# A two-layer gated encoder in fp32 on one core: a third plain block at the FFN's start, one-bank PSUM tiles for half products, other buffers and orders in the way down

## The chip, the cores and the metric

The kernel runs on one core of a Trainium2 chip. The metric is the device time of one execution in microseconds (us), the median of several runs. In a profile PE is TensorE (matmuls), PEld its weight loads, DVE is VectorE, ACT ScalarE, POOL GpSimd and SP SyncE; the last issues most of the DMAs. A core's matrix products go into PSUM, which has eight banks of 512 fp32 values in each of 128 partitions.

## The reference

Two sequences of 512 and 256 tokens with 1024 features go through two layers. A layer adds a mixer of four gated branches to x and then a feed-forward network (FFN) with a short convolution over the tokens. What bears on the change is the end of the mixer and the FFN:

```python
for l in range(2):
    ...
    x = x + merged @ w_out[l]                      # 1024 x 1024
    h = rms_norm(x, ffn_norm[l])
    u = depthwise_conv(h @ w_up[l], w_dw, b_dw)    # 1024 x 5632, three taps over tokens
    a, b = split(u)                                # 2816 columns each
    x = x + (silu(a) * b) @ w_down[l]              # 2816 x 1024
```

All of it is fp32. The kernel makes an fp32 product of three passes, with each operand split in a high part and a remainder.

## The kernel before, in words

Both sequences lie side by side as 768 columns (tokens); features lie on the 128 partitions, so x is eight tiles of 128 x 768. HALF is 384. A product of K blocks of 128 features takes 3K matmuls for each column segment (`fm`, L488): high by high, remainder by high, high by remainder. Weights come in units of 128 x 512 by DMA (`raw`, issued by SP), are rounded on ACT (`whi`, L434) and the remainder taken on DVE (`wlo`, L443).

PSUM tiles are of two kinds: `mm_ps()` gives a tile of two banks (two of them), `ps()` a tile of one bank (four of them). A tile is taken again when its last reader is done.

`proj_out` (the way out of the mixer): x tiles 0 to 3 get a full product each; tiles 4 to 7 get their product in two rounds, first columns 0 to 383, then 384 to 767. Products 0 and 1 of a round share a two-bank tile, and so do 2 and 3. DVE adds each to x (L1413). Behind each round `hnorm` normalises that half: squares on ACT, sums on POOL, column sums and a broadcast by two small matmuls on PE (L580, L592), then for each of the eight tiles a scaling (L602) and a split into `hh` (ACT, L616) and `hl` (DVE, L618).

The FFN has 22 blocks j, each a pair of 128-column products (columns j and 22 + j of w_up), which go through the convolution (L1443 on ACT, L1437 and L1439 on DVE, four DVE rows for a product), tanh (L1547), a DVE step (L1549), a multiplication on POOL (L1550) and a split (L1552 on ACT, L1554 on DVE). The pairs are of two kinds:

- A plain block is two products over all 1024 features and both halves: 96 matmuls of 384 columns. Blocks 0 and 1 are plain (`ffn_plain`). While PE does them, `t_gen` and `t3_gen` make the inputs T1 to T4 of the other kind on DVE and ACT, from the normalised x. ACT copies each half product out of PSUM (L1457).
- The others go by Strassen-like sums, seven half products for the pair (`ffn_seven`): 84 matmuls. The first, X, is copied out (L1510) and accumulated into again. The seventh (T4) is put off to `ffn_rest`, which runs inside the next pair behind its second product, or inside a way down.

`FF_SEQ` is the order of pairs ("u", j) and ways down ("d", first block, blocks): a way down multiplies two or four finished blocks by their rows of w_down, for all eight x tiles. Each result is copied to a `y` buffer (L1585; three buffers) and added to x in DRAM (`xsp`) by an accumulating DMA that POOL issues (L1564). A way down of two blocks is eight products of 12 matmul pairs. The last way down of a layer takes x from DRAM and adds on the chip: in layer 0 in two rounds by `lagged` (columns 0 to 511, then 512 to 767; DVE adds at L1372 and next layer's norm work follows), in layer 1 by a whole product, an addition (L1603) and a store (L1604) for each x tile.

The instruction order on each engine is fixed at build time by a planner's clock: generators queued with a due time (`go_fast`) put their instructions in when PE's counted time passes it. `b()` gives a tile of 128 x 768 from a pool of 24, `s()` one of six.

Of the kernel before, what the change touches and what calls it, by code (L numbers as in the profile page):

```python
# [21 lines left out]
SEQS = ((0, 4), (4, 2))  # L22
GATE_ORDER = (2, 1, 3, 0)
NFF = 22
FF_PLAIN = 2
HALF = NT // 2

FF_SEQ = (("u", 0), ("u", 1), ("u", 2), ("u", 3), ("d", 0, 2), ("u", 4), ("u", 5), ("u", 6), ("d", 2, 4), ("u", 7),
          ("u", 8), ("u", 9), ("u", 10), ("d", 6, 4), ("u", 11), ("u", 12), ("u", 13), ("u", 14), ("d", 10, 4),
          ("u", 15), ("u", 16), ("u", 17), ("u", 18), ("u", 19), ("d", 14, 2), ("u", 20), ("u", 21), ("d", 16, 2),  # L30
          ("d", 18, 4))
# [216 lines left out]
class Net:  # L248
# [1139 lines left out]
    def proj_out(self):  # L1388
        nc = self.nc
        self.xs = []  # L1390
        self.norm_begin()
        self.xg = {0: [], HALF: []}
        src = self.xin if self.l == 0 else self.xsp
        for m in range(8):
            x = self.b()
            nc.sync.dma_start(out=x, in_=src[m])
            self.xs.append(x)
        for m in range(8 - self.LAG):
            p = self.mm_ps()
            self.fm(self.halves(p), self.units(2, 128), self.mg, rel=4)  # L1400
            self.add_x(p, self.xs[m], m)
            self.sq_in(m, self.xs[m], 0, HALF)
            self.sq_in(m, self.xs[m], HALF, NT)
            self.go_fast(self.save_x(m, self.xs[m], 0, NT), 2.0)
        jobs = [(m, self.units(2, 128)) for m in range(8 - self.LAG, 8)]
        for c0 in (0, HALF):
            for i, (m, us) in enumerate(jobs):
                if i % 2 == 0:
                    p = self.mm_ps()
                pp = p[:, 512 * (i % 2):512 * (i % 2) + HALF]  # L1410
                self.fm(((pp, c0, c0 + HALF),), us, self.mg, 4 if c0 else 0)
                x = self.xs[m][:, c0:c0 + HALF]
                nc.vector.tensor_add(x, x, pp)  # L1413
                self.sq_in(m, self.xs[m], c0, c0 + HALF)
                self.go_fast(self.save_x(m, self.xs[m], c0, c0 + HALF), 1.5)
            self.hnorm(c0, 3.0, self.f("fn"))

    def lagged(self, jobs, g, fin):

        self.drain()  # L1420
        for c0, c1 in ((0, NS), (NS, NT)):
            for i, (m, us, xs, x, rel) in enumerate(jobs):
                if i % 2 == 0:
                    pp = self.mm_ps()
                p = pp[:, 512 * (i % 2):512 * (i % 2) + 512]
                self.fm(((p[:, 0:c1 - c0], c0, c1),), us, xs, rel if c0 else 0)
                self.x_update(p[:, 0:c1 - c0], x, m, g, c0, c1)
                fin(m, x, c0, c1)
# [30 lines left out]
    def ffn_plain(self):  # L1459
# [1 line left out]
        cols = [c + j for j in range(FF_PLAIN) for c in (0, NFF)]  # L1461
        n = 3
        wts = [self.units(2, 128) for _ in cols]
        zs = [self.b() for _ in cols]
        self.finish(0)
        for w, z in zip(wts[:n], zs):
            self.plain_half(z, 0, w)
# [12 lines left out]
        self.run_out(e)  # L1480
        for j in range(FF_PLAIN):
            self.go_fast(self.ffn_block(j, *zs[2 * j:2 * j + 2]), 1.0 + 9.0 * j)

    def ffn_block(self, j, z1, z2):
        u = []
# [71 lines left out]
    def ffn(self):  # L1557
# [10 lines left out]
        for step in FF_SEQ[FF_PLAIN:]:  # L1568
# [8 lines left out]
            if step != FF_SEQ[-1]:  # L1577
                for m in range(8):
# [2 lines left out]
                    if o == 0:  # L1581
                        us = self.units(1, 128)
                    self.fm(self.full(p), us, xs, n * int(o + n == 4), o)
                    y = self.pm.tile([128, NT], F32, tag="y", name=self.nm("y"), bufs=3)
                    nc.scalar.copy(y, p[:, 0:NT])  # L1585
                    self.go_fast(add(m, y), 1.0)
                    if o + n == 4:
                        self.ffn_rest()
                continue
            self.ffn_rest()  # L1590
            self.drain()
# [6 lines left out]
            if last_l:  # L1598
                self.drain()
                for m in range(8):  # L1600
                    p = self.mm_ps()
                    self.fm(self.full(p), self.units(1, 128), xs, 4)
                    nc.vector.tensor_add(xx[m], xx[m], p[:, 0:NT])  # L1603
                    nc.sync.dma_start(out=self.out[m], in_=xx[m])  # L1604
                continue
            jobs = [(m, self.units(1, 128), xs, xx[m], 4) for m in range(8)]
            self.norm_begin()
# [135 lines left out]
```

## Time and profile before

| | |
|---|---|
| runs, us | 2838.42, 2837.56, 2827.6; median 2837.56 |
| profiled execution, us | 2834.98, its span 2833.2 |
| busy, us of the span | PE 2729.4 (96%), DVE 1781.7 (63%), ACT 1151.5 (41%), POOL 689.7 (24%) |
| mean granted clock of PE | 0.984 of full speed |

Busy times are sums over instructions; a matmul's end is modelled, so PE's 96% is not 96% of its best rate. An engine's idle time costs something only where PE waits for it.

### The profile page before, as it was taken

To read this page: it belongs to the slowest core of one execution; us is meant where nothing else is said; L and a number is where in the kernel's file an instruction comes from. 1 tells how busy PE (TensorE), PEld (TensorE's weight loads), DVE (VectorE), ACT (ScalarE), POOL (GpSimd) and SP (SyncE) were. 2 spreads that over 40 slices of the span, in tenths; PEclk is the share of its full clock that TensorE was granted. 3 is DMA by queue.
4 is the path that set the end of the run, shared out by engine and by line. 5 is a ranking of instruction groups with operands and counts; after the bars stand their busy time and mean duration, and the time that the engine had idled before them with its cause. 6 is when DMAs were issued, how large, how long until landed. Compare 5 with 4: busy or idle time off the path is not lost. (4 is left out here: it accounts for less than half of the span.)

```text
span 2833.2 us, 40110 instructions
## 1 busy us (share of the span) xinstructions
PE 2729.4 (96%) x15196; PEld 2468.4 (87%) x15196; DVE 1781.7 (63%) x3046; ACT 1151.5 (41%) x2349; POOL 689.7 (24%) x584
## 2 busy tenths in 40 slices
PE   9999999999998899999899999999999988999999
PEld 8778988888898799998787789888888987999988
DVE  6644347786338767868546443477864386678674
ACT  6443333223225445545444433332232254455452
POOL 3402113121121332233215021131211213322331
PEclk9999999999999999999999999999999999999999
DMA  4101113221141454344621111131212413543445
GB/s 161 42 27 38 43 48 114 61 67 60 60 143 48 88 117 96 97 101 113 171 90 42 27 38 42 49 114 60 67 60 60 140 51 87 118 96 97 102 108 156
DMA packets 129793, 233.71 MB, mean 82 GB/s; under 512 B 18496, under 2 KB 36288, under 8 KB 129600
## 3 DMA queue, kind: packets, MB, share of 16 engines
q1 hardware_dynamic: 115776, 193.40, 21.6%
q0 software_dynamic: 13824, 37.75, 8.2%
q8 instruction: 119, 1.95, 0.3%
q14 instruction: 74, 0.61, 0.1%
HBM read 174.33 MB, written 55.20 MB: 81 GB/s over the span
## 5 line engine op out<-in xcount | busy, mean ns | idle before, releaser
L443 DVE TENSOR_TENSOR wlo<-raw,whi 128x512 fp32r<-128x512 f32 (+1 forms) x576 | 456.4, 798 | 116.6 <-ACT whi L434 97.7
L488 PE MATMUL mm<-b,whi 128*128 128x256 f32 (+2 forms) x1920 | 439.9, 343 | 39.1 <-DVE b L1554 13.7
L434 ACT CAST whi<-raw 128x512 fp32r<-128x512 f32 (+1 forms) x576 | 346.4, 613 | 232.2 <-PE mm L488 79.6
L488 PE MATMUL ps<-b,whi 128*128 128x384 f32 (+1 forms) x1472 | 362.4, 342 | 32.6 <-ACT s L1510 26.0
L488 PEld LDWEIGHTS mm<-b,whi 128*128 128x128 f32 x1920 | 315.7, 192 | 77.7 <-DVE b L1554 16.2
L512 PE MATMUL mm<-whi,hh 128*128 128x512 f32 (+2 forms) x752 | 312.4, 415 | 6.8 <-ACT hh L537 5.7
L488 PE MATMUL mm<-hh,whi 128*128 128x512 f32 (+1 forms) x1152 | 302.1, 343 | 0.0
L488 PEld LDWEIGHTS ps<-b,whi 128*128 128x128 f32 x1472 | 255.3, 191 | 48.2 <-ACT s L1510 28.0
L488 PE MATMUL mm<-hh,wlo 128*128 128x512 f32 (+1 forms) x1152 | 296.8, 338 | 0.0
L488 PE MATMUL mm<-hl,whi 128*128 128x512 f32 (+1 forms) x1152 | 294.8, 337 | 0.0
L512 PE MATMUL mm<-whi,hl 128*128 128x512 f32 (+2 forms) x752 | 278.8, 371 | 0.3 <-DVE hl L544 0.2
L512 PE MATMUL mm<-wlo,hh 128*128 128x512 f32 (+2 forms) x752 | 278.2, 370 | 0.0
L488 PE MATMUL ps<-hh,whi 128*128 128x384 f32 x768 | 259.2, 338 | 7.3 <-ACT s L1516 4.4
L488 PE MATMUL mm<-b,wlo 128*128 128x512 f32 (+2 forms) x960 | 264.5, 340 | 0.0
L488 PE MATMUL ps<-hl,whi 128*128 128x384 f32 x768 | 258.9, 337 | 1.3 <-DVE hl L618 1.3
L488 PE MATMUL ps<-hh,wlo 128*128 128x384 f32 x768 | 257.7, 336 | 0.0
L519 POOL TENSOR_TENSOR st<-st,mhalf 128x16 f32<-128x16 f32 (+5 forms) x50 | 94.9, 1897 | 599.0 <-DVE st L1002 374.7
L488 PE MATMUL ps<-b,wlo 128*128 128x384 f32 (+1 forms) x736 | 230.2, 341 | 0.0
L1356 POOL TENSOR_TENSOR b<-b,b 128x768 f32<-128x768 f32 x48 | 100.2, 2087 | 463.4 <-DVE b L1351 447.1
L512 PEld LDWEIGHTS mm<-whi,hh 128*128 128x128 f32 x752 | 177.1, 236 | 29.2 <-issue 12.8
L488 PEld LDWEIGHTS mm<-hh,whi 128*128 128x128 f32 x1152 | 177.3, 189 | 26.6 <-issue 3.3
L488 PEld LDWEIGHTS mm<-hh,wlo 128*128 128x128 f32 x1152 | 176.2, 188 | 24.4
(230 smaller groups left out, 4811.9 us busy)
## 6 DMA issues: line engine op xcount, KB each, us to landing
raw<-wu SPq DMA_DIRECT2D x560, 256.0 KB, 2.7
xsp<-y POOLq DMA_DIRECT2D x96, 384.0 KB, 6.0
b<-xsp SPq DMA_DIRECT2D x24, 384.0 KB, 6.0
do<-ot SPq DMA_DIRECT2D x36, 132.0 KB, 1.8
b<-do SPq DMA_DIRECT2D x12, 384.0 KB, 3.5
raw<-wu SPq DMA_DIRECT2D x16, 208.0 KB, 4.0
b<-xin SPq DMA_DIRECT2D x8, 384.0 KB, 6.5
xsp<-b SPq DMA_DIRECT2D x8, 384.0 KB, 2.5
```

The source lines that it names most:

```text
L434: self.nc.scalar.copy(hi, raw)
L443: self.nc.vector.tensor_sub(lo, raw, hi.bitcast(F32))
L488: nc.tensor.matmul(ap, w, x[:, c0:c1], start=(k == 0 and i == 0 and not more), stop=(k == K - 1 and i == 2), skip_group_check=more)
L512: nc.tensor.matmul(ap, x[:, cols], w, start=(k == 0 and i == 0), stop=(k == 7 and i == 2))
L519: self.nc.gpsimd.tensor_tensor(r, ms, self.mhalf[:, 0:n], op=ALU.pow)
L1356: nc.gpsimd.tensor_add(a, a, t)
```

## The change

The third block becomes plain: `FF_PLAIN` is 3, and in `FF_SEQ` the first way down comes behind pair 4 in place of pair 3. The two products of block 2 lie in two of the three `y` buffers. In `proj_out` and `lagged` every half product gets a one-bank tile. `ffn_rest` is called behind every product of a way down; it does something at the first call only, so in a way down of two blocks the put-off seventh product comes behind the first x tile, before behind the second. In the last way down but one, d(16, 2), copies 1 to 7 go to `b()` tiles. In layer 1 the last two x tiles are finished, added and stored in two pieces, 512 and 256 columns.

```diff
-FF_PLAIN = 2
+FF_PLAIN = 3
...
-FF_SEQ = (("u", 0), ("u", 1), ("u", 2), ("u", 3), ("d", 0, 2), ("u", 4), ("u", 5), ("u", 6), ("d", 2, 4), ("u", 7),
+FF_SEQ = (("u", 0), ("u", 1), ("u", 2), ("u", 3), ("u", 4), ("d", 0, 2), ("u", 5), ("u", 6), ("d", 2, 4), ("u", 7),
...
             for i, (m, us) in enumerate(jobs):
-                if i % 2 == 0:
-                    p = self.mm_ps()
-                pp = p[:, 512 * (i % 2):512 * (i % 2) + HALF]
+                pp = self.ps()[:, 0:HALF]
...
             for i, (m, us, xs, x, rel) in enumerate(jobs):
-                if i % 2 == 0:
-                    pp = self.mm_ps()
-                p = pp[:, 512 * (i % 2):512 * (i % 2) + 512]
+                p = self.ps()
...
-        zs = [self.b() for _ in cols]
+        zs = [self.b() for _ in cols[:4]] + [self.y() for _ in cols[4:]]
...
-                    y = self.pm.tile([128, NT], F32, tag="y", name=self.nm("y"), bufs=3)
+                    y = self.b() if step == FF_SEQ[-2] and m else self.y()
                     nc.scalar.copy(y, p[:, 0:NT])
                     self.go_fast(add(m, y), 1.0)
-                    if o + n == 4:
-                        self.ffn_rest()
+                    self.ffn_rest()
...
+                    for c0, c1 in ((0, NS), (NS, NT)):
+                        p = self.ps()
+                        self.fm(((p[:, 0:c1 - c0], c0, c1),), w, xs, 4 * int(c0 > 0))
+                        nc.vector.tensor_add(xx[m][:, c0:c1], xx[m][:, c0:c1], p[:, 0:c1 - c0])
+                        nc.sync.dma_start(out=self.out[m, :, c0:c1], in_=xx[m][:, c0:c1])
```

Below `FF_PLAIN` the lines of the changed kernel lie a few lines lower or higher (L1411 for L1413, L1453 for L1457, L1584 for L1585, L1563 for L1564, L1549 for L1550, L1546 for L1547, L1551 for L1552). In the order of instructions the change shows as follows; behind a row stands whose semaphores it waits for (`Activation` is ACT). First PE in layer 0's second round of `proj_out`: the ones-matmul of the first half's norm, the starts of products 2 and 3 (tiles `mm` or `ps`, `b` is the merged branches, `whi` the weights), and the first plain product (from `hh` and `hl`). Before:

```order
L592 MATMUL ps_7763<-s_7749,ones 128x384 [waits DVE_49]
...
L488 MATMUL mm_7773<-b_6634,whi_7412 128x384
L488 MATMUL mm_7773<-b_6635,whi_7412 128x384
...
L488 MATMUL mm_7773<-b_6634,whi_7481 128x384 [waits DVE_49]
L488 MATMUL mm_7773<-b_6635,whi_7481 128x384
...
L488 MATMUL ps_7893<-hh_7256,whi_7550 128x384 [waits DVE_49,Activation_49]
```

And now:

```order
L592 MATMUL ps_7766<-s_7752,ones 128x384 [waits DVE_49]
...
L488 MATMUL ps_7776<-b_6634,whi_7412 128x384 [waits PE_49]
L488 MATMUL ps_7776<-b_6635,whi_7412 128x384
...
L488 MATMUL ps_7830<-b_6634,whi_7481 128x384
L488 MATMUL ps_7830<-b_6635,whi_7481 128x384
...
L488 MATMUL ps_7899<-hh_7256,whi_7550 128x384 [waits DVE_49,Activation_49]
```

Product 3 has a tile of its own and no wait for DVE; the order is the same.

Second, ACT in the first way down of two blocks: the copies into y (`DMASW` is a wait for one of the accumulating stores, counted from the first), with what stands between them. Before:

```order
L1585 COPY y_8588<-mm_8562 128x768 [waits PE_49]
L434 CAST whi_8603<-sum_8518 128x512 [waits DVE_49]
L1585 COPY y_8606<-mm_8590 128x768 [waits PE_49]
L434 CAST whi_8625<-raw_8434 128x512
L1536 ACTIVATE s_8398<-ps_8399 128x384 [waits PE_49]
L1443 ACTIVATE s_8641<-s_8398,fc_80 128x768 [waits DVE_49,Activation_49]
L1585 COPY y_8653<-mm_8628 128x768 [waits PE_49]
L434 CAST whi_8668<-raw_8480 128x512 [waits DMAHW4_49,DVE_49]
L1547 ACTIVATE s_8398<-s_8561 128x768 [waits DVE_49,Activation_49]
L1585 COPY y_8674<-mm_8655 128x768 [waits DMASW0_49,PE_49]
L1585 COPY y_8698<-mm_8676 128x768 [waits DMASW1_49,PE_49]
```

And now:

```order
L1546 ACTIVATE y_7894<-s_8628 128x768 [waits DVE_49,Activation_49]
L1584 COPY y_8737<-mm_8708 128x768 [waits PE_49]
...
L1535 ACTIVATE s_8532<-ps_8533 128x384 [waits PE_49]
L1439 ACTIVATE s_8768<-s_8532,fc_80 128x768 [waits DVE_49,Activation_49]
...
L1584 COPY y_8782<-mm_8757 128x768 [waits PE_49]
L1551 ACTIVATE b_8729<-y_7894 128x768 [waits Pool_49]
L1546 ACTIVATE s_8532<-s_8707 128x768 [waits DVE_49,Activation_49]
L1584 COPY y_8809<-mm_8784 128x768 [waits DMASW0_49,PE_49]
L434 CAST whi_8824<-raw_8614 128x512 [waits DMAHW0_49]
L1584 COPY y_8829<-mm_8811 128x768 [waits DVE_49,PE_49]
L1584 COPY y_8851<-mm_8831 128x768 [waits DMASW1_49,PE_49]
```

`y_7894` is a product of block 2, which is still being gated. The wait for the first store stands at the third copy, one sooner, and the fourth waits for DVE's last step on `y_7894`.

Third, POOL in the last way down but one, d(16, 2) of layer 0: the stores and the multiplication of the last block. Before:

```order
L1564 DMA xsp<-y_12553 128x768 [waits DMASW0_49,Activation_49]
L1564 DMA xsp<-y_12571 128x768 [waits DMASW1_49,Activation_49]
L1564 DMA xsp<-y_12616 128x768 [waits DMASW2_49,Activation_49]
L1550 TENSOR_TENSOR s_12377<-s_12377,s_12604 128x768 [waits DVE_49,Pool_49]
L1564 DMA xsp<-y_12637 128x768 [waits DMASW3_49,Activation_49]
```

And now:

```order
L1563 DMA xsp<-y_12548 128x768 [waits DMASW0_49,Activation_49]
L1563 DMA xsp<-b_12591 128x768 [waits DMASW1_49,Activation_49]
L1549 TENSOR_TENSOR s_12372<-s_12372,s_12577 128x768 [waits DVE_49,Pool_49]
L1563 DMA xsp<-b_12614 128x768 [waits DMASW2_49,Activation_49]
L1563 DMA xsp<-b_12634 128x768 [waits DMASW3_49,Activation_49]
```

The multiplication stands one store sooner, and the stores from the second on read tiles of the large pool.

## Rows read from the trace of the kernel before

**Rows 1.** PE's waits, whole span: us in total, times, longest us
```profile
PE ps L488 <- ACT s L1510: 26.0, 6, 5.5
PE mm L488 <- DVE b L1554: 13.7, 8, 2.8
PE mm L488 <- DVE b L1413: 10.1, 8, 2.9
...
PE mm L488 <- ACT y L1585: 6.5, 4, 3.6
PE mm L488 <- DVE b L1372: 5.9, 8, 1.2
...
PE ps L488 <- DVE b L1413: 2.9, 2, 2.1
```

**Rows 2.** Busy time by engine in one stretch of layer 0's FFN
```profile
core 0: us, PE busy (x) PEld busy (x) DVE busy (x) ACT busy (x) POOL busy (x), PEclk, DMA share, GB/s
895.50:938.30 42.80, 31.28 (x166) 29.60 (x164) 40.48 (x62) 24.61 (x43) 10.13 (x6) 0.96 0.18 56
```

**Rows 3.** The same of three short stretches (PEclk: granted clock)
```profile
850.30:857.10 6.80, 6.00 (x19) 6.00 (x20) 6.80 (x10) 3.47 (x7) 3.30 (x2) 0.50 0.21 65
1379.40:1382.80 3.40, 3.05 (x8) 1.86 (x6) 0.31 (x1) 0.80 (x1) 0.85 (x1) 0.50 1.08 281
2267.40:2274.20 6.80, 4.46 (x24) 4.14 (x24) 6.80 (x11) 3.53 (x7) 3.29 (x2) 1.00 0.23 68
```

**Rows 4.** PE in order of time, way out of the mixer
```profile
851.10 1.01 PE L488 MATMUL mm<-b,whi 128*128 128x384 f32 x2 [2.91 <-DVE b L1413]
```

**Rows 5.** DVE in order of time, the same place
```profile
845.62 1.70 DVE L602 SCALAR_TENSOR_TENSOR b<-b,fc,ssq 128x384 f32<-128x384 f32 x2 [0.42 <-ACT ssq L596]
...
858.35 0.56 DVE L1413 TENSOR_TENSOR b<-b,mm 128x384 f32<-128x384 f32 x1 [1.25 <-PE mm L488]
...
859.35 1.84 DVE L618 TENSOR_TENSOR hl<-b,hh 128x384 fp32r<-128x384 f32 x2
```

**Rows 6.** PE in order of time: layer 0's first pairs, kernel's end
```profile
897.53 0.51 PE L488 MATMUL ps<-b,whi 128*128 128x384 f32 x2
...
904.64 0.79 PE L488 MATMUL ps<-b,whi 128*128 128x384 f32 x2 [4.86 <-ACT s L1510]
...
938.29 0.62 PE L488 MATMUL mm<-b,whi 128*128 128x512 f32 x2 [2.79 <-DVE b L1554]
...
2794.55 0.98 PE L488 MATMUL mm<-b,whi 128*128 128x512 f32 x4 [0.89 <-ACT y L1585]
```

**Rows 7.** DVE in order of time: behind layer 0's plain products
```profile
904.42 0.74 DVE L1437 SCALAR_TENSOR_TENSOR s<-b,fc,s 128x511 f32<-128x511 f32 x1
...
906.78 0.69 DVE L443 TENSOR_TENSOR wlo<-sum,whi 128x512 fp32r<-128x512 f32 x1
...
914.73 2.35 DVE L1437 SCALAR_TENSOR_TENSOR s<-b,fc,s 128x511 f32<-128x511 f32 x1
...
937.30 0.94 DVE L1554 SCALAR_TENSOR_TENSOR b<-b,b 128x768 fp32r<-128x768 f32 x1
```

**Rows 8.** ScalarE (ACT) in order of time, layer 0, ahead of pair 5
```profile
977.04 1.03 ACT L1443 ACTIVATE s<-s,fc 128x768 f32<-128x768 f32 x1
980.61 0.48 ACT L1510 COPY s<-ps 128x384 f32<-128x384 f32 x1 [2.54 <-PE ps L488]
```

**Rows 9.** GpSimd (POOL) in order of time, a block's multiplication
```profile
914.29 2.23 POOL L1550 TENSOR_TENSOR b<-b,s 128x768 f32<-128x768 f32 x1 [13.89 <-DVE b L1549]
```

**Rows 10.** Line L1585 (ns min/median/max), and landings of L1564 stores
```profile
L1585 ACT COPY y<-mm x96: 774/800/804, 941.6 to 2797.5; 128x768 f32<-128x768 f32 x96
...
DMA to landing us min/median/max: 4.3/6.0/10.5
```

**Rows 11.** DMA issues: KB each, median us to landing
```profile
out<-b SPq DMA_DIRECT2D x8, 384.0 KB, 2.3
...
xsp<-b SPq DMA_DIRECT2D x8, 128.0 KB, 1.7
```

More of the change, by code (lines that the diff above doesn't have):

```diff
@@ L1482, in ffn_plain, with y @@
             self.go_fast(self.ffn_block(j, *zs[2 * j:2 * j + 2]), 1.0 + 9.0 * j)
+    def y(self):
+        return self.pm.tile([128, NT], F32, tag="y", name=self.nm("y"), bufs=3)
     def ffn_block(self, j, z1, z2):
@@ L1600, in ffn @@
                 for m in range(8):
[L1601 to L1604, printed above, removed]
+                    w = self.units(1, 128)
+                    if m < 6:
+                        p = self.mm_ps()
+                        self.fm(self.full(p), w, xs, 4)
+                        nc.vector.tensor_add(xx[m], xx[m], p[:, 0:NT])
+                        nc.sync.dma_start(out=self.out[m], in_=xx[m])
+                        continue
+                    for c0, c1 in ((0, NS), (NS, NT)):
[3 more added lines that the diff above has]
+                        nc.sync.dma_start(out=self.out[m, :, c0:c1], in_=xx[m][:, c0:c1])
                 continue
```

## The prediction

> **What bounds the kernel now.** I read the list of waits first, then the stretches around the two FFN openings, then single rows. TensorE (PE) is busy nearly all the time, so what counts is where it waits. Its list of waits [rows 1] names, for both layers together: 26.0 us for the copy of L1510 (a pair's first product leaving PSUM), 13.7 for L1554 (the last step of a gated block), 10.1 and 2.9 for the additions of L1413 (the way out of the mixer), 6.5 for the copies of L1585 (the way down) and 5.9 for L1372 (the end of a layer). All of these places are edited. Around 860 to 980 us, where layer 0 opens its FFN, the waits have one cause at a time. From the end of the plain products (first matmul of the next product but one at 897.53 less the 2.1 us of the product before it, so 895.45) to 938.3 PE is busy 31.3 of 42.8 us and VectorE (DVE) 40.5 [rows 2]: there DVE is the bound. Three stretches show what a wait costs beyond itself: PE ran at half clock (0.50) for 6.8 us after the 2.9 us wait at 851.10 [rows 4] and for 3.4 us near 1379, but not after the same wait in layer 1 (1.00) [rows 3]. A half-clock stretch costs half of PE's busy time in it: 3.0 and 1.5 us.
>
> The sum is made against the profiled execution, 2835.0 us (span 2833.2 and 1.8 around it). The median of the three runs, 2837.6, is 2.6 above it, inside their own spread of 10.8. About 0.5%, 14 us, is what a measurement of this kernel can tell from no change.
>
> **A. Half products of the way out in one-bank tiles.** Today products 1 and 3 of each round write the second half of a tile whose first half DVE still has to read. Eight waits cost 10.1 us, the longest (one per layer) 2.9, so the other six 0.72 on average [rows 1]. With a tile for each product, PE goes on at once; what it then meets is the normalised input of the first plain product. That chain runs on DVE from 845.62 to 861.2, 1.25 us of it waiting for PE's last product [rows 5], and is set off by a ones-matmul on PE, ahead of which three short waits (2.1 us) go. So it would run from 843.5 for 14.3 us to 857.8; the first plain product, whose last eighth and six one-column matmuls take about 0.9 us more, ends at 858.7. Before it starts when the addition at 858.35 ends and takes 24 matmuls and those six. One matmul takes 0.173 us: from 897.53 to the start of the wait that ends at 904.64 there are 2.25 us, less 0.17 for the last one's end, for twelve [rows 6]. That gives 863.8. Layer 0 gains 5.1. Layer 1 has no half clock to win (3.0 less) but a longer wait at the hand-over, 2.1 against 0.8 of the 2.9 [rows 1], so 1.3 more: 3.4. **A: -8.5**, between -4.3 (only the six short waits) and -16 (all of 10.1, 2.9 and 3.0).
>
> **B. A third plain block.** A pair by seven products takes 84 matmuls, plain 96. Twelve more at 0.173 are +2.1 us a layer. Against it stands the bound of the opening. DVE cannot start the first convolution before the plain products are done; today it starts 9.0 us behind them, at 904.42, as the transformed inputs (T1 to T4) still occupy DVE and ScalarE. From there it takes 33.8 us to the end of the L1554 at 937.30 that the first product of the way down needs [rows 7]; PE passes at 938.29 [rows 6]. With 16.6 us more plain products, the transformed inputs are ready before PE is; the first convolution starts 1.5 us behind PE (a copy and a 1.0 us scaling on ScalarE, [rows 8]). The same DVE work lies ahead of the way down, two pairs by seven and two blocks, and one more set of convolution rows of the third block, 2.4 us (904.42 to 906.78, [rows 7]). So 1.5 + 33.8 + 2.4 = 37.7 in place of 42.8: -5.1, net of the matmuls -3.0 a layer. **B: -6.0**, between +4.2 (DVE's lateness stays whole) and -24 (PE never waits there: 28 us in place of 42.8).
>
> POOL slows DVE in that stretch: while it multiplied from 914.29 to 916.5 [rows 9], the DVE row at 914.73 took 2.35 us in place of 0.74 [rows 7]. The Trainium skill (SBUF — State Buffer, "Who interferes with whom") has it that a DVE instruction with two SBUF inputs stands still for the whole of a GpSimd one that reads SBUF; the trace agrees, as that row ends 0.6 behind POOL's. By this rule a third block's multiplication in the same stretch would cost up to 2.2 us more a layer, and B would be -1.6; by the instruction order it falls behind the L1554 that counts, so B stays.
>
> **C. The third block's inputs lie in two of the three y buffers.** The way down of blocks 0 and 1 has eight copies into y, each followed by an accumulating store. Before, the fourth copy waits for the first store; now the third does, and the fourth for DVE to end block 2. Call the moment when PE passes the wait for L1554 R. Before, R = 938.3, and the X product of the pair after next ends as its copy starts, 980.6 [rows 8], so starts at 978.5; less the 14.6 us of the pair between, the way down with its stalls takes 25.6. Now POOL's queue has block 2's multiplication ahead of the first store. DVE reaches what that needs after some 15 rows, about 9 us (four of them the convolution set); POOL's multiplication takes 2 [rows 9], so the first store goes at R + 11 and lands 6.0 later, and the third copy (0.8) is over at R + 18 [rows 10]. PE, which without it would have needed the tile at R + 10, stands for 8 us, and has five products and copies still to go: the pair starts at R + 27. **C: +2.8** for both layers. Least: 0 waits, 16.6 us, -18. Most: a landing of 10.5 [rows 10] and a new half-clock stretch of 3.0, +18.
>
> **D. The seventh product one product sooner** is neutral in the other short way down, d(14,2): POOL's multiplication also moves one place up, ahead of the third store in place of behind it, so that store leaves later as the block is ready sooner; the y buffers go on setting the pace. 0, up to 2 us either way in a layer.
>
> **E. y copies of d(16,2) in the large pool.** Copies 1 to 7 no longer wait for a store. Of the 6.5 us for L1585, 3.6 (the longest [rows 1]) stand in layer 0 ahead of the last way down, followed by the half clock at 1379 (1.5 [rows 3]), and 0.9 in layer 1 [rows 6]. L1554 of the last pair, the next thing that PE needs, comes sooner too (it stood behind such a copy on ScalarE). **E: -6.0**, at least -2 if the loads of x, which need the stores, come late instead.
>
> **F. One-bank tiles at the end of layer 0**: 5.9 us of L1372 [rows 1] go. DVE's additions and splits take about as long as the 256-column products there, but four tiles let PE run ahead. **F: -5.9**, -3 to -9 (a half-clock stretch behind it may go as well).
>
> **G. Split last stores.** Behind the last matmul stand an addition of 768 columns, about the 0.94 us of the DVE row of that size at 937.30 [rows 7], and a store of 384 KB, 2.3 us. A third of the columns is left: 0.6 off the addition, and by the 128 KB row, 1.7, another 0.6 off the store [rows 11]. **G: -1.2**.
>
> **Sum**: -8.5 - 6.0 + 2.8 - 6.0 - 5.9 - 1.2 = -24.8; 2835.0 - 24.8 = 2810.
>
> **Rivals.**
> *The y buffers cost more.* For it speaks that stores in the way down have taken up to 10.5 us to land [rows 10] and that an 8 us stall is longer than any at these places so far (5.5 at most [rows 1]); against it, that the old stall at the next pair's X goes, which C counts. +7.5 us a layer on C: 2825.
> *DVE's lateness stays.* DVE is 40.5 of 42.8 busy and the third block brings it a full block of convolution and gating. If the first convolution is again 9 us late, B is +4.2: 2820. Against: the transforms run while PE has 16.6 us more to do.
> *All waits go.* If the block's y buffers come free in time and the first plain product finds its input, A, B and C go half of the way to their far ends, some -25 us more: 2785.
> *Slower.* If two y buffers stayed taken for the whole way down, each of the eight copies would wait for its predecessor's store, 0.8 + 6.0 = 6.8 us [rows 10], 54 us in place of 25.6, +29 a layer: 2866 with the other terms. It decides from about five such copies a layer: each costs 4.7 us more than PE's 2.1, the old way down has 9 us over its 16.6 to give, and the other terms 13.8 a layer. Against it: in the changed queue only the third and fourth copies wait on something new.
>
> **How the numbers follow.** Chances: forecast (2797 to 2822) 0.58; y buffers 0.16; DVE's lateness 0.12; all waits gone 0.09; slower 0.05. Faster by over 0.5% means below 2823.4: the forecast, all waits gone, most of DVE's lateness and a quarter of the y case, 0.80; within 0.5%: 0.15; slower 0.05. The range 2792 to 2826 leaves out the slower case, half of the all-gone case and some of the y case's far side, under 0.2. The likeliest case's own range is 2797 to 2822.
>
> **What would show it.** A: no PE wait for the additions of the way out, small waits for hl in the first plain product. B: the first convolution within 2 us of the last plain copy, and d(0,2) ready some 5 us sooner after the plain products. C: a PE wait of about 8 us for a y copy in the middle of d(0,2), none at the next pair's X. E, F: no PE wait for L1585 in d(16,2), none for x additions at the layer's end. Wrong it would be if the stall of C were twice as long, or if new half-clock stretches followed the small waits of A.

## The result, and the profile after

The changed kernel takes 2803.4 us (median of four runs, 2801.5 to 2810.3); the kernel before, run beside it, 2833.3 (2827.6 to 2838.4). The ratio is 0.990, 95% interval 0.987 to 0.9929. The profiled execution took 2802.0 with a span of 2800.2, so the span fell by 33.0 us against the profiled execution of before; the medians are 29.9 apart.

PE's waits over the whole span now (us in total, times, longest), to be held against [rows 1]:

```profile
PE ps L488 <- DVE s L1524: 17.8, 8, 3.6
PE mm L488 <- DVE b L1553: 12.3, 6, 2.7
PE ps L488 <- ACT whi L434: 8.5, 2, 4.2
PE mm L488 <- ACT y L1584: 7.3, 4, 2.8
PE ps L488 <- ACT s L1515: 7.1, 2, 3.6
...
PE mm L512 <- DVE b L1372: 1.9, 1, 1.9
...
PE ps L488 <- DVE hl L618: 1.2, 6, 0.2
```

The 26.0 us for the copy of L1510 (now L1509) are gone, as are the 13.0 for the additions of the way out and the 5.9 for L1372 at the end of layer 0 (the row of 1.9 is another wait, at the start of layer 1; it was 1.13). New are 8.5 us at the first plain product, and there is more for L1515 (4.4 before, 7.1 now) and for L1524 (6.6 before, 17.8 now), the row with which DVE takes a pair's T3 product out of the PSUM tile into which the put-off seventh product then accumulates. In order of time, layer 0's opening on PE (in brackets the wait ahead of the row and who ended it):

```profile
852.81 0.66 PE L488 MATMUL ps<-hh,whi 128*128 128x384 f32 x1 [4.23 <-ACT whi L434]
...
937.63 0.69 PE L488 MATMUL ps<-hh,whi 128*128 128x384 f32 x1 [3.58 <-ACT s L1515]
946.74 0.85 PE L488 MATMUL mm<-b,whi 128*128 128x512 f32 x2 [2.67 <-DVE b L1553]
951.80 1.01 PE L488 MATMUL ps<-b,whi 128*128 128x384 f32 x2 [3.57 <-DVE s L1524]
...
965.66 0.61 PE L488 MATMUL mm<-b,whi 128*128 128x512 f32 x2 [2.80 <-ACT y L1584]
```

Busy time by engine: the first plain product's start, the plain products' end to the first way down, and that way down (to be held against [rows 2] and [rows 3]):

```profile
core 0: us, PE busy (x) PEld busy (x) DVE busy (x) ACT busy (x) POOL busy (x), PEclk, DMA share, GB/s
851.40:858.20 6.80, 5.39 (x17) 5.42 (x18) 4.04 (x7) 1.97 (x4) 1.16 (x1) 0.50 0.08 30
908.35:946.74 38.39, 31.84 (x166) 30.59 (x165) 36.80 (x54) 21.64 (x33) 9.72 (x6) 0.91 0.20 62
946.74:974.09 27.35, 20.97 (x101) 18.18 (x101) 21.65 (x27) 15.44 (x23) 12.32 (x10) 0.81 0.54 102
```

R, the moment when PE passes the wait for L1553, comes 38.4 us behind the plain products, forecast 37.7, and the next pair 27.35 us behind R, forecast 27. The first convolution on DVE starts 2.8 us behind the plain products, forecast 1.5; before it was 8.8:

```profile
911.27 0.74 DVE L1433 SCALAR_TENSOR_TENSOR s<-b,fc,s 128x511 f32<-128x511 f32 x1
```

Still DVE is busy 36.8 of the 38.4 us: read so, the opening has its pace from DVE.

To say where the time went, I cut each layer at places that all kernels have: the start of the half products of the way out, the end of the first plain product, the starts of d(2, 4), d(14, 2), d(16, 2) and the last way down, and that one's end. Each cut is the start (or end) of a matmul in order of time, matched to its product by counting L488 matmuls through the instruction order; a length is the difference of two. Layer 0 / layer 1, us:

```
                              before       changed      two_plain    rest_second  late_block_40  late_block_pool
way out to 1st plain's end    49.5 / 48.2  46.6 / 45.7  47.9 / 46.8  45.7 / 46.7  45.7 / 45.4    43.3 / 42.3
  to the start of d(2,4)     143.3 /144.2 140.8 /140.8 139.8 /139.7 141.4 /141.6 135.3 /135.1   137.6 /135.2
  to d(14,2)                 296.1 /296.0 295.3 /295.3 298.2 /296.5 299.0 /295.7 295.7 /295.3   295.3 /298.8
  to d(16,2)                  52.0 / 54.6  52.4 / 52.3  52.0 / 54.0  52.0 / 58.4  52.6 / 53.8    53.4 / 53.1
  to the last way down        22.5 / 19.8  18.7 / 18.7  18.7 / 18.7  18.7 / 18.7  18.7 / 18.7    18.7 / 18.7
  to its end                  48.5 / 34.2  37.7 / 33.5  36.2 / 33.5  36.2 / 33.5  37.7 / 33.5    36.2 / 33.5
```

For the changed kernel: 5.4 us at the first plain product, 5.9 in the opening, 1.5 up to d(14, 2), 2.0 around it, 4.8 in d(16, 2), 11.5 in the last ways down and 1.3 behind the last matmul (4.5 to 3.2), together 32.4 of the 33.0.

Each column is one profiled execution, and half-clock stretches differ between executions. rest_second, below, does the same as the changed kernel from the way out to the end of the first plain product; yet that cut differs by 0.9 and 1.0 us. Between d(2, 4) and d(14, 2), where both meet waits of the same length, it is 3.7 us longer in layer 0: behind the same wait of 1.76 us for L1553 in d(6, 4) the granted clock was 0.50 (1.2 GHz of 2.4) in rest_second, the first row, and 1.00 in the changed kernel (columns as above):

```profile
1097.20:1100.40 3.20, 3.20 (x12) 3.18 (x11) 2.76 (x5) 1.27 (x2) 0.87 (x1) 0.50 0.24 20
1099.10:1102.30 3.20, 3.20 (x21) 3.08 (x20) 3.06 (x6) 2.21 (x4) 0.88 (x1) 1.00 0.24 20
```

So a difference of a few us in one cut may be the clock's alone; it counts for more where both layers and several kernels agree.

### The profile page after: what moved, and what is told of

It reads as the page before. It is cut to its first block, busy times and chain, and to the rows that moved or that the text cites. A ratio compares the mean times of both kernels' runs of the same rounds, so it can differ in the third digit from the quotient of the medians.

```text
span 2800.2 us, 40105 instructions
## 1 busy us (share of the span) xinstructions
PE 2721.9 (97%) x15220; PEld 2469.6 (88%) x15220; DVE 1778.9 (64%) x3032; ACT 1150.0 (41%) x2343; POOL 679.9 (24%) x580
## 5 line engine op out<-in xcount | busy, mean ns | idle before, releaser
L443 DVE TENSOR_TENSOR wlo<-raw,whi 128x512 fp32r<-128x512 f32 (+1 forms) x576 | 464.9, 813 | 116.2 <-ACT whi L434 96.8
L488 PE MATMUL ps<-b,whi 128*128 128x384 f32 (+2 forms) x1840 | 454.3, 340 | 17.8 <-DVE s L1524 17.8
L488 PEld LDWEIGHTS ps<-b,whi 128*128 128x128 f32 x1840 | 320.7, 191 | 36.2 <-DVE s L1524 20.7
L488 PE MATMUL mm<-b,whi 128*128 128x512 f32 (+1 forms) x1504 | 327.6, 339 | 19.6 <-DVE b L1553 12.3
L488 PE MATMUL mm<-hh,whi 128*128 128x512 f32 (+1 forms) x1152 | 301.7, 343 | 0.0
L488 PE MATMUL mm<-hh,wlo 128*128 128x512 f32 (+1 forms) x1152 | 295.5, 337 | 0.0
L488 PE MATMUL mm<-hl,whi 128*128 128x512 f32 (+1 forms) x1152 | 294.4, 336 | 0.0
L488 PE MATMUL ps<-b,wlo 128*128 128x384 f32 (+2 forms) x920 | 291.1, 339 | 0.0
L488 PE MATMUL ps<-hh,whi 128*128 128x384 f32 x800 | 272.0, 340 | 15.6 <-ACT whi L434 8.5
L488 PEld LDWEIGHTS mm<-b,whi 128*128 128x128 f32 x1504 | 239.5, 190 | 48.2 <-DVE b L1553 14.9
L488 PE MATMUL ps<-hl,whi 128*128 128x384 f32 x800 | 271.4, 339 | 1.2 <-DVE hl L618 1.2
L488 PE MATMUL ps<-hh,wlo 128*128 128x384 f32 x800 | 270.4, 338 | 0.0
L512 PEld LDWEIGHTS mm<-whi,hh 128*128 128x128 f32 x752 | 177.2, 236 | 29.9 <-issue 13.6
L488 PEld LDWEIGHTS mm<-hh,whi 128*128 128x128 f32 x1152 | 176.7, 188 | 26.0 <-issue 3.4
L488 PEld LDWEIGHTS mm<-hl,whi 128*128 128x128 f32 x1152 | 175.7, 188 | 24.7
L488 PEld LDWEIGHTS mm<-hh,wlo 128*128 128x128 f32 x1152 | 175.8, 188 | 24.4
```

The costliest lines, as they stand in the source:

```text
L443: self.nc.vector.tensor_sub(lo, raw, hi.bitcast(F32))
L488: nc.tensor.matmul(ap, w, x[:, c0:c1], start=(k == 0 and i == 0 and not more), stop=(k == K - 1 and i == 2), skip_group_check=more)
L512: nc.tensor.matmul(ap, x[:, cols], w, start=(k == 0 and i == 0), stop=(k == 7 and i == 2))
```

## The experiments

The first theory was the prediction's: each term stands for itself, so undoing or mending one gives its price. Its rival, which the 36.8 of 38.4 us suggest: the opening is one chain on DVE, and a wait removed on PE comes back later on the way.

**One PSUM pool.** The new wait of 4.2 us carries the name of ACT's rounding of weights. Ahead of the first plain product these rows stand in order of time, first on DVE, then on ACT of the changed kernel:

```profile
852.12 0.54 DVE L1411 TENSOR_TENSOR b<-b,ps 128x384 f32<-128x384 f32 x1
...
853.12 1.83 DVE L618 TENSOR_TENSOR hl<-b,hh 128x384 fp32r<-128x384 f32 x2
```

```profile
852.18 0.61 ACT L434 CAST whi<-raw 128x512 fp32r<-128x512 f32 x1
```

The product waits for semaphores of both engines. The mixer and the FFN each open PSUM pools of their own, and in the instruction order the count for which it waits on DVE is that of the L1411 at 852.12, which reads another bank (5; the product's is 0). The edit:

```diff
-        with self.tc.tile_pool(name=name, bufs=1) as self.pm, \
-                self.tc.tile_pool(name=name + "ps", bufs=1, space=bass.MemoryType.PSUM) as self.pps:
+        with self.tc.tile_pool(name=name, bufs=1) as self.pm:
...
+        self.pps = pool("ps", space=bass.MemoryType.PSUM)
```

> The changed kernel with one PSUM pool for all phases (before: mixer and FFN each open their own). Theory: the one wait of 4.2 us (layer 0) and 4.25 us (layer 1) ahead of the first plain product is for the last addition of the way out (DVE, 852.12), because the FFN's pool opens only when the mixer's pool is done with, not for an input of the product. Then the first plain product starts behind the way out at once, meets waits under 1 us for its inputs, ends near 856 in place of 860.4, layer 1 the same, and the wait of 1.9 us at the start of layer 1 goes too: 8 to 11 us less, 2793 to 2796. Rival: the profile's own name for the wait, ACT's rounding of weights that ends at 852.8, holds PE: the wait stays and the time is that of the changed kernel, 2803.

Measured: 2804.1 us, ratio 0.9882 (0.9861 to 0.9903). PE in order of time:

```profile
852.39 0.45 PE L488 MATMUL ps<-hl,whi 128*128 128x384 f32 x1 [0.81 <-DVE hl L618]
...
853.85 0.45 PE L488 MATMUL ps<-hl,whi 128*128 128x384 f32 x1 [0.67 <-DVE hl L618]
...
945.44 0.61 PE L488 MATMUL mm<-b,whi 128*128 128x512 f32 x2 [3.92 <-DVE b L1553]
950.51 1.01 PE L488 MATMUL ps<-b,whi 128*128 128x384 f32 x2 [4.11 <-DVE s L1524]
```

The theory is right about the wait (it was the pool; ACT's name was wrong) and wrong about the time. The first plain product ends 43.4 us behind the way out's halves in both layers, 3.2 and 2.3 less, with the small waits for hl that the prediction wanted; but the waits for L1553 and L1524 grow from 2.7 and 3.6 to 3.9 and 4.1, and from the way out to d(2, 4) it is 188.9 and 186.2 us against 187.4 and 186.5. (The gain is 3.2 in layer 0 and 2.3 in layer 1; two expectations below name the two the other way round.) The 1.9 us at the start of layer 1 went as well, but from layer 0's end to layer 1's way out it takes 805.7 us, the changed kernel 805.5.

**Block 2 in the large pool.**

```diff
-        zs = [self.b() for _ in cols[:4]] + [self.y() for _ in cols[4:]]
+        zs = [self.b() for _ in cols]
```

> The changed kernel with block 2's two products in tiles of the large pool in place of two y buffers. Theory: the stall of 2.8 us (layer 0) and 2.7 us (layer 1) for the fourth copy into y in d(0,2) goes, nothing else moves: 2797 to 2799. Rival: large-pool tiles that come free later hold DVE or ACT instead (the gated blocks take theirs from the same pool), and the stall of 3.6 us for the first product of the way down grows by what is saved: 2803 or more.

Measured: 2806.2 us, 0.989 (0.9868 to 0.9912). The rival's outcome: in layer 0 the 2.8 us wait breaks up into 0.8, 0.3 and 1.2 and the wait for L1553 grows to 3.8 (in layer 1 to no more than 2.8), and from the first plain product's end to d(2, 4) it is 141.1 and 141.2 us, no less than with the y buffers (140.8).

**The seventh product where it was.**

```diff
-                    self.ffn_rest()
+                    if o + n == 4:
+                        self.ffn_rest()
```

> The changed kernel with the put-off seventh product behind the second product of a way down of two, as before the change. Theory (term D was mis-sized): placed behind the first product it finds its PSUM tile not yet read by DVE (L1524), 3.6 and 3.5 us in d(0,2) and d(14,2) of each layer with half clock behind it; a product later the wait is 1.5 us, as in d(14,2) before: 2 to 3.5 us less at four places, 2789 to 2796. Rival: what is saved there comes back as the waits that the early place took away, 2.75 us and half clock for the X copy of the pair behind d(14,2) and the y copies: 2801 to 2805.

Measured: 2812.5 us, 0.9914 (0.9893 to 0.9935), its profile 7.1 us longer than that of the changed kernel. The rival is right in kind: the wait for L1524 falls to 1.5 us in d(14, 2), and waits for copies come back. Its price is larger than it said: 6.1 us of the profile stand around d(14, 2) of layer 1, 58.4 us against 52.3. But in layer 0 the same place takes 52.0 against 52.4, and 3.7 us stand between d(2, 4) and d(14, 2), most of it the clock (above). POOL in d(14, 2) of layer 1, first in this kernel, then in the changed one:

```profile
2711.01 1.27 POOL L425 TENSOR_TENSOR sum<-raw,raw 128x512 f32<-128x512 f32 x1 [5.21 <-DMA raw<-wu]
2714.03 2.16 POOL L1549 TENSOR_TENSOR s<-s,s 128x768 f32<-128x768 f32 x1 [1.74 <-DVE s L1548]
2716.14 2.65 POOL L1563 DMA_DIRECT2D xsp<-y  x3
```

```profile
2708.24 1.86 POOL L1549 TENSOR_TENSOR s<-s,s 128x768 f32<-128x768 f32 x1 [2.08 <-DVE s L1548]
2710.04 0.85 POOL L1563 DMA_DIRECT2D xsp<-y  x1
```

With the seventh product a place later, the late block's multiplication stands on POOL one store later, and three stores stand behind it. It starts 20.5 us behind the start of d(14, 2), at 2714.0; in layer 0 of this kernel 17.6, in the changed kernel 15.7 in both layers. So the place is worth 1.9 of the 4.8 us. The other 2.9 are a late load of weights: it landed 8.9 us after its issue, 6.0 at the same place in layer 0, and POOL's sum (L425) and DVE's rows behind it waited for it. The three stores leave together at 2716.1. ACT in this kernel, then PE:

```profile
2720.94 0.80 ACT L1584 COPY y<-mm 128x768 f32<-128x768 f32 x1 [3.87 <-DMA xsp<-y]
...
2724.42 0.80 ACT L1584 COPY y<-mm 128x768 f32<-128x768 f32 x1 [2.17 <-DMA xsp<-y]
...
2725.64 0.48 ACT L1509 COPY s<-ps 128x384 f32<-128x384 f32 x1
```

```profile
2726.17 1.01 PE L488 MATMUL ps<-b,whi 128*128 128x384 f32 x2 [5.61 <-ACT s L1509]
```

The last two copies into y wait for these stores, and the X copy of the next pair stands behind them: PE waits 5.61 us for it, 2.57 in layer 0.

The kernel before has the same kind of wait. Of its 26.0 us for L1510, 16.3 stand in the pairs behind the four ways down of two, and in each of the four one or two of the last copies into y waited 0.9 to 3.7 us for a store ahead of the X copy. In d(0, 2) of layer 0, ACT, then PE:

```profile
965.36 0.80 ACT L1585 COPY y<-mm 128x768 f32<-128x768 f32 x1 [2.58 <-DMA xsp<-y]
966.58 0.48 ACT L1510 COPY s<-ps 128x384 f32<-128x384 f32 x1
```

```profile
967.11 1.01 PE L488 MATMUL ps<-b,whi 128*128 128x384 f32 x2 [5.49 <-ACT s L1510]
```

So these were waits for late stores two queues away. The Trainium skill (PSUM — Partial Sum Buffer, "Engine vs sequencer instructions") says that the queues of ScalarE, VectorE and GpSimd are strictly first in, first out; the rows agree: in both kernels the X copy starts 0.4 us after the last y copy ends, with one cast between them.

**Two plain blocks.** `FF_PLAIN = 2` and the old `FF_SEQ` in the changed kernel.

> The changed kernel with two plain blocks and the old order of pairs, all else kept. Theory (terms B and C as the trace shows them): from the plain products' end to the first way down 42.8 us again in place of 38.4, the pair by seven in place of the plain one gives 2.1 us back a layer, way down equal; 5 to 8 us more than the changed kernel, 2808 to 2811. Rival: DVE's lateness is only moved, the third plain block is worth nothing or costs its 2.1 us a layer: 2799 to 2804.

Measured: 2803.9 us, 0.9888 (0.9864 to 0.9912). The rival: the third plain block is worth nothing beside the other edits. From the first plain product's end to d(2, 4) the kernel without it is even 0.9 and 1.1 us shorter, but its first plain product ends that much later; from the way out it is 187.8 and 186.4 us against 187.4 and 186.5. Without the early seventh product (rest_second against before) the same edits B and C do give 1.9 and 2.6 us; the early seventh product alone (two_plain against before) 3.5 and 4.5; both together 2.5 and 3.4. About 1 us of each of these is A's (the kernel without A, below, has 141.9 and 142.0 in this cut). Read so, they are two ways to the same gain; the differences are near what the clock alone can make, and the early seventh product without A was not run.

**A later first way down.** In the changed kernel, pair 5 ahead of d(0, 2); the same with one pool; and the changed order with two plain blocks.

```diff
-... ("u", 3), ("u", 4), ("d", 0, 2), ("u", 5), ("u", 6), ("d", 2, 4), ...
+... ("u", 3), ("u", 4), ("u", 5), ("d", 0, 2), ("u", 6), ("d", 2, 4), ...
```

> The changed kernel with pair 5 ahead of d(0, 2) in place of behind it. The four runs before this one gave the same time within 3 us whether the way out's wait of 4.2 us, the y stall of 2.8 us or the third plain block was taken away; only the place of the seventh product told. Theory: from the plain products to the first way down DVE's chain of late blocks is the bound, and a wait removed ahead of it comes back at the wait for L1553 or right behind it. Then 12.5 to 14.6 us more of PE's work ahead of the way down gives DVE the time: the four waits there (3.6, 2.7, 3.6 and 2.8 us a layer) and the half clock behind them (17 us of it in layer 0) mostly go, 8 to 18 us a layer, 2768 to 2788. Rival: tiles of the large pool run out (two more for block 5 with none given back), the gating of blocks 3 to 5 waits for d(0, 2), and the waits stand as long as now or appear at d(2, 4): 2795 to 2812.

> The same with one PSUM pool for all phases as well. Theory: with DVE's lateness in the opening gone, the 2.3 us (layer 0) and 3.2 us (layer 1) that the one pool wins up to the end of the first plain product are no longer given back at the first way down: 4 to 6 us less than the kernel with pair 5 ahead of d(0, 2) alone. Rival: DVE still is the bound there: same time.

> The changed kernel with two plain blocks, but the changed order, so that three pairs by seven (2, 3 and 4) stand ahead of d(0, 2). It tells the third plain block apart from the place of the way down. Theory: what counts is how much of PE's work lies ahead of the first way down, 14.6 us more than with the old order: the waits for L1553 and behind it in d(0, 2) go, the wait of 4.9 us for the first X copy stays (nothing ahead of it changes): 4 to 9 us a layer less, 2786 to 2796. Rival: DVE's work per PE time is the same for either kind of block, so that the lateness at the way down stays what it is: 2800 to 2806.

Measured: 2815.2 us, 0.9925 (0.9908 to 0.9942); 2813.9, 0.9918 (0.9896 to 0.994); 2811.8, 0.991 (0.9893 to 0.9928). The kernel before took 2838.6 beside these and the next one, 2 to 7 us more than beside the others, so the ratios count. All three miss my theory, and the second is its rival's case. The first and third have larger ratios than the changed kernel, with intervals that overlap its own; by the traces the first takes 191.1 and 190.5 us from the way out to d(2, 4), the third 188.4 and 189.2, the changed kernel 187.4 and 186.5. In the first the wait for L1553 goes, but those for L1515 and L1524 grow to 5.7 and 4.9 us. Plain products' end to the way down, pair 5 ahead of it:

```profile
909.19:966.70 57.51, 46.86 (x241) 45.58 (x241) 55.00 (x77) 30.95 (x48) 15.04 (x8) 0.91 0.20 60
```

DVE is busy 55.0 of 57.5 us: with one more pair DVE gets its work as well as PE, and stays as late as it was. In the way down DVE has less to do (21.7 of 27.4 us busy in the changed kernel, with the backlog), so there it can catch up. Putting the way down off did not help.

**The way out in two-bank tiles** (edit A undone alone in the changed kernel).

```diff
-                pp = self.ps()[:, 0:HALF]
+                if i % 2 == 0:
+                    p = self.mm_ps()
+                pp = p[:, 512 * (i % 2):512 * (i % 2) + HALF]
```

> The changed kernel with the two-bank tiles of before in the way out of the mixer (edit A undone alone). Theory: the eight waits of 10.1 us come back, the first plain product ends 2.5 to 3 us later in each layer, but the opening behind it has its pace from DVE, whose chain starts no earlier: of A's 5.3 us little is kept at the start of d(2, 4), 2803 to 2806. Rival (A as in the prediction): all of it is kept: 2808 to 2812.

Measured: 2811.8 us, 0.9908 (0.9894 to 0.9923), which the interval does not tell from 0.990; the trace does. From the way out to d(2, 4) it is 190.2 and 189.0 us, 2.9 and 2.5 more: as far as these cuts tell, all of A is kept, the rival's side. (Another 4.0 us of the profile's difference lie between d(2, 4) and d(14, 2), where A does nothing.) With one pool's failure this says where DVE's chain begins: A lets PE finish the way out sooner, so DVE's own work starts sooner; one pool moved PE alone. From the start of the half products to the end of the last split of that half (L618) it takes 45.4 and 44.1 us here, 41.2 in the changed kernel and 41.2 with one pool.

**Block 2 later on DVE.** If DVE is the bound, what counts is which rows stand ahead of those that PE waits for. DVE in the changed kernel, around R:

```profile
940.40 1.78 DVE L1433 SCALAR_TENSOR_TENSOR s<-y,fc,s 128x511 f32<-128x511 f32 x1
...
945.73 0.95 DVE L1553 SCALAR_TENSOR_TENSOR b<-b,b 128x768 fp32r<-128x768 f32 x1
...
948.84 0.74 DVE L1433 SCALAR_TENSOR_TENSOR s<-y,fc,s 128x511 f32<-128x511 f32 x1
...
951.20 0.55 DVE L1524 TENSOR_TENSOR s<-s,ps 128x384 f32<-128x384 f32 x1
```

Two sets of four rows on y (block 2, not needed before d(2, 4)) stand ahead of the L1553 and of the L1524 that PE waits for. The edit, with block 2 in the large pool so that it may lie longer:

```diff
-            self.go_fast(self.ffn_block(j, *zs[2 * j:2 * j + 2]), 1.0 + 9.0 * j)
+            self.go_fast(self.ffn_block(j, *zs[2 * j:2 * j + 2]), 1.0 + 9.0 * j if j < 2 else 40.0)
```

> The changed kernel with block 2's two products in tiles of the large pool and its convolution and gating queued 40 us behind the plain products in place of 19, so that on DVE they stand behind the rows that the first way down waits for. Theory: from the plain products' end DVE is busy 36.8 of 38.4 us and is the bound; block 2 is not needed before d(2, 4), yet 3.4 us of its rows stand ahead of the L1553 that the way down waits for and 2.4 us ahead of the L1524 that the seventh product waits for. Moved behind, the waits of 2.7, 3.6 and 2.8 us fall below 1 each, with part of the half clock: 6 to 12 us a layer, 2780 to 2792. Rival: the rows only collide with pairs 5 and 6, whose own rows are then late for d(2, 4): the waits stand there, 2800 to 2808.

The second kernel, no_conv, leaves out all 24 convolution rows of the three plain blocks on DVE:

```diff
-            yield from self.ffn_u(u[-1], z, col)
+            self.ffn_mid(u[-1], z, col)
+            yield 1.3
```

> The changed kernel without the twelve rows of DVE a layer for each of the two outer taps of the convolution of the three plain blocks (24 rows, 14.4 us a layer; the output lacks these taps). Theory (DVE is the bound in the opening): the waits between the plain products and the end of d(0, 2) (12.6 us and 17 us of half clock in layer 0) go but for the first, 3.6: 12 to 18 us a layer, 2767 to 2780. Rival (PE waits there for ScalarE's copies, POOL or the landings of stores, and DVE is only busy beside them): under 4 us a layer, 2795 to 2803.

Measured: late_block_40 2793.1 us, 0.9864 (0.9839 to 0.989); no_conv 2788.8, 0.9847 (0.9818 to 0.9876). PE in late_block_40:

```profile
941.63 0.80 PE L488 MATMUL mm<-b,whi 128*128 128x512 f32 x1 [2.81 <-DVE b L1553]
944.33 1.01 PE L488 MATMUL ps<-b,whi 128*128 128x384 f32 x2 [1.05 <-DVE s L1524]
...
962.12 0.97 PE L488 MATMUL mm<-b,whi 128*128 128x512 f32 x4 [0.27 <-ACT y L1584]
```

From the first plain product's end to d(2, 4) late_block_40 is 5.4 and 5.7 us shorter than the changed kernel, just short of the 6 to 12 expected; against z_in_b, from which it differs in the order alone, 5.8 and 6.1. The waits for L1515, L1524 and y fall to 2.2, 1.1 and 0.3 in layer 0; the wait for L1553 stays, and two of 1.4 and 1.2 us (L1551, the next X copy) come to stand beside it. Leaving the rows out gives 7.8 and 8.4 (133.0 and 132.4 us) of the 14.4 that they take, less than the 12 to 18 expected and more than the rival's 4. Plain products' end to R in no_conv:

```profile
909.87:941.25 31.38, 28.59 (x166) 28.15 (x165) 25.46 (x34) 21.51 (x33) 9.79 (x6) 1.00 0.24 76
```

DVE is then busy 25.5 of 31.4 us and no longer the bound. So DVE is what binds the opening, for about 8 us a layer. PE still waits 2.8 us for L1553 there, with DVE free; what that wait hangs on (a chain over ACT, POOL and DVE through one block, as I take it) I have not taken apart.

**Both together, and the ends alone.** late_block_pool is late_block_40 with one PSUM pool; ends_alone is the kernel before with edits E, F and G.

> The kernel with block 2 late and in the large pool, and one PSUM pool for all phases as well. Theory: with the opening less late on DVE, part of the 2.3 and 3.2 us that the one pool wins at the first plain product is kept, and the wait at the start of layer 1 (1.9 us) goes: 3 to 6 us less than without it, ratio 0.984 to 0.985. Rival: DVE's chain from the last addition of the way out to the first way down still has the say, and only the wait at the layer's start counts: 0 to 2 us less, ratio 0.9857 to 0.9864.

> The kernel of before with edits E, F and G alone (copies of d(16, 2) in the large pool, one-bank tiles at the end of layer 0, split last stores). Theory (the terms as the trace shows them): 3.7 and 1.1 us in d(16, 2), 10.8 at the end of layer 0 with the half clock, 0.7 in the last way down, 1.3 behind it: 17.6 us less than before, ratio 0.9938. Rival (the prediction's terms): 6.0, 5.9 and 1.2, so 13.1 us, ratio 0.9954; or part of it is given back at the start of layer 1, where DVE's norm work then ends last: 10 us or less, ratio above 0.9965.

Measured: late_block_pool 2789.1 us, 0.9835 (0.9815 to 0.9854), the fastest whole kernel here; ends_alone 2819.1, 0.9941 (0.9922 to 0.9961). In late_block_pool the cut from the way out to d(2, 4) is 180.9 and 177.5 us against 181.0 and 180.5 in late_block_40: one pool is kept in layer 1 and not in layer 0. The median is 4.0 us lower than late_block_40's, within the theory's 3 to 6, but the two intervals overlap; of the 4.3 us between the profiles this cut holds 3.1.

ends_alone gives 16.7 us by its ratio, with an interval of about 5.5 to either side: it agrees with the terms of the trace (17.6) and does not exclude the prediction's 13.1. Its trace does tell: d(16, 2), the last ways down and what stands behind the last matmul are together 17.8 us shorter than before. At the start of layer 1 the wait is 0.8 us longer (1.93), no more.

## Why the prediction was right, step by step

The range (2792 to 2826, around 2810) holds 2803; the sum of -24.8 us was -33.0 between the two profiles and -29.9 between the medians. Inside the sum two terms were wrong in mechanism, B and D, and nearly cancel: that the time fits is in part luck. (Three bounds are off by their own terms: B's far end is -25.4, "all waits go" 2787, "slower" 2864. Neither the range nor a chance moves by it.)

**A, forecast -8.5: -5.4, mis-sized.** The first plain product ends 2.9 and 2.5 us earlier, not 5.1 and 3.4. DVE's chain was done sooner than forecast (854.95, forecast 857.8; 0.9 of it because all of layer 0 ran that much earlier). The step that failed is "PE goes on at once; what it then meets is the normalised input": PE met the end of the mixer's PSUM pool. It stood still for 4.2 us in place of working beside the chain, and the half clock, counted as gone, came back behind that wait (0.50 from 851.4 to 858.2, and for 3.4 us from 2250.8 in layer 1, where before there was none). One pool shows the forecast's picture, 6.0 and 4.8 us at that cut. That A's gain is kept to d(2, 4) is what undoing it shows.

**B, forecast -6.0, and C, +2.8: nothing beside D.** R behind the plain products fell from 42.8 to 38.4 us, nearly as forecast, and the next pair came at R + 27.35, as forecast. But two_plain is as fast. The step that failed is the comparison of B alone with before: it counted as B's what the early seventh product gives by itself. In C the third copy into y came nearly when forecast (it ran from 964.81 to R + 18.9, forecast R + 18), but PE came to need its tile at R + 16 and not R + 10: it had waited 3.6 us for L1524, which the prediction did not name, and run at half clock (0.50 from 946.9 to 957.2), so the stall for y was 2.8 and not 8. z_in_b shows that it has no price of its own. Also, I took 14.6 us for the pair behind the old way down, which has only six of its seven products in that stretch: before, 27.7 and not 25.6 is what stands against 27.35. (A way down of two is 96 matmuls, eight products of 12, not of 12 pairs; the 2.1 us a product in C fits that.)

On POOL in that stretch the prediction weighed a rule of the Trainium skill (SBUF — State Buffer, "Who interferes with whom"): a DVE instruction with two SBUF inputs contends with a GpSimd one that reads SBUF. Block 2's multiplication fell behind R, at 957.12, as the instruction order said, so it does not bear on R; where it did run, the trace agrees with the rule, as the L1433 at 957.63 took 2.28 us in place of 0.74 (POOL, DVE):

```profile
957.12 2.24 POOL L1549 TENSOR_TENSOR y<-y,s 128x768 f32<-128x768 f32 x1 [8.76 <-DVE y L1548]
```

```profile
957.63 2.28 DVE L1433 SCALAR_TENSOR_TENSOR s<-s,fc,s 128x511 f32<-128x511 f32 x1
```

**D, forecast 0: some -6 alone in the opening (3.5 and 4.5 less A's 1 each), the main miss.** "The y buffers go on setting the pace" looked at d(14, 2) and at the third store alone. In d(0, 2) what counts is when the multiplication on POOL lets the stores behind it go, and so the X copy two queues on. In d(14, 2) the X copy's wait of 2.75 us goes too, but the wait for L1524 grows from 1.5 to 3.5, and the forecast of 0 holds: the changed kernel is 0.4 us slower in layer 0. The 2.4 by which it is faster in layer 1 are the clock: before, the same wait for the X copy (2.75 and 2.77 us) was followed by 6.8 us at 0.50 in layer 1 (from 2748.1) and by full clock in layer 0.

**E, forecast -6.0: -6.3.** d(16, 2) takes 18.7 us in both layers, 3.7 and 1.1 less, and the half clock of 1.5 behind it is gone. **F, -5.9: -8.5**, within its bounds: 10.8 us in the last way down of layer 0, less the 1.5 of E, less 0.8 more wait at the start of layer 1 (1.13 to 1.89). A half-clock stretch of 6.8 us (from 1416.9 before) went too, as the prediction allowed for, and one of 3.4 us came (from 1397.5); two_plain and rest_second, without it, take 36.2 us there in place of 37.7. **G, -1.2: -1.3.**

**The rivals.** None came as stated. "DVE's lateness stays" asked for a first convolution 9 us late again, and it was 2.8; yet its outcome for B, no gain, is what two_plain shows, and DVE is as busy after the change as before. It gave 2820 because it took B's loss without D's gain. The y buffers cost less, not more; "all waits go" and "slower" did not happen.

## What to carry to other kernels

Where an engine was busy 96% of a stretch, a wait taken from another engine in that stretch came back further on; what helped was to start the busy engine's chain sooner (A), or to put what nobody waits for behind what somebody does (block 2: 10 us for one number, and tiles in another pool, which alone gave nothing). When a step is moved, follow all that it issues through each queue that runs in order: here a multiplication ahead of three stores on POOL decided when ScalarE could copy for PE. A wait for several engines needs a second look before it is named: the profile named ACT, and the cause was a pool's end on DVE. And a cut of a few us is held against a second run of the same code before it is read: here the clock alone made 1 to 3.7 us.

## What the runs showed of the hardware

The accumulating stores that POOL issues differ in their time to landing with the way down. In the changed kernel those of d(16, 2) from the large pool, which leave without waiting for a buffer, land in 9.0 us (median), the others in 4.9:

```profile
xsp<-y POOLq DMA_DIRECT2D x82, 384.0 KB, 4.9
...
xsp<-b POOLq DMA_DIRECT2D x14, 384.0 KB, 9.0
```

PE did not wait for them: d(16, 2) takes 18.7 us in both layers, and the last ways down follow at once. DVE did: the loads of x wait for these stores, and the first addition of layer 0's last way down came 5.2 us late for its x. PE, with four one-bank tiles to fill, ran on meanwhile.

```profile
1372.78 0.69 DVE L1372 TENSOR_TENSOR b<-b,ps 128x512 f32<-128x512 f32 x1 [5.24 <-DMA b<-xsp]
```

Behind a wait of one and the same length PE's granted clock fell to 0.50 in one execution and stayed at 1.00 in another: behind 1.76 us in d(6, 4) of rest_second and of the changed kernel, and behind 2.77 and 2.75 us in the two layers of the kernel before.
